# Two lead-ins of a hybrid block: single PSUM banks, and the last chunk's norm set step by step among the weights' splits

## The chip, the cores and the metric

One core of a Trainium2 chip runs the kernel. The metric is the device time of one execution in microseconds (us); the median of three runs before the change is 2560.94, from 2557.63 to 2561.89.

## The reference

One layer of a trunk with three sub-layers on x of shape [1, 1024, 1024] in float32. Each is normalised before and after, and added to the stream:

```python
x = x + rms_norm(merged @ w_mix_out[l], g_post_mix[l])
h = rms_norm(x, g_pre_xa[l])
mem_n = rms_norm(mem, g_mem[l])
x = x + rms_norm(memory_cross_attention(h, mem_n, w_xq[l], w_xkv[l], w_xo[l]), g_post_xa[l])
h = rms_norm(x, g_pre_ffn[l])
x = x + rms_norm(swiglu(h, w_gu[l], w_down[l]), g_post_ffn[l])
```

`merged` is a stick-breaking attention and a Mamba-2 mixer, gated and summed. `memory_cross_attention` begins with the query projection `h @ w_xq`, and `swiglu` with `h @ w_gu`, 1024 to 2 x 2816. The change is about the places where an output projection, a post-norm, an addition and a pre-norm run into one of these two products.

## The kernel before, in words

The engines are TensorE (PE, matmul), VectorE (DVE), ScalarE (ACT), GpSimd (POOL) and SyncE (SP, which issues most transfers). Matrices are split into a high part and a low part of reduced precision (`hi` is made by ACT, `lo` by DVE as the difference), and each product is three matmuls: high by high, high by low, low by high. A weight tile of 128 output columns and half of the 1024 inputs thus needs 12 matmuls of 128x128 by 128x512; this is `acc3`, called a product below.

**The chunks.** `out_proj` (L1453) multiplies the activations by an output projection in chunks of 128 rows, 8 in all, four to a half of the sequence. For each chunk it loads the old x, makes the product in a two-bank PSUM tile (tag `p2`), squares and sums it on ACT (L1469), turns the sum into a scale on POOL (`rstd_of`, L173 and L174), scales by it and by the gain on DVE (L1471, "the first scaling"), adds the old x (L1472), and stores the new x. `pre_norm` (L178) then does a second square (L181) and a second scaling (L182) for the sub-layer that follows, and returns a function that transposes the chunk on PE (8 transposes) and one, `put`, that moves the transposes into the blocks that the next products need (L1513 for the second half: two copies on ACT, six operations on DVE). The list `late` holds these back so that the transposes of a chunk follow the product of the next.

**The scheme of the products.** The next sub-layer's matmul is done by a Winograd-Strassen scheme: of each weight block with quarters a11, a12, a21, a22 it makes combinations s1 = a21 + a22, s2 = s1 - a11, s3 = a11 - a21, s4 = a12 - s2, and of the activations blocks b11, b21, b22, t1, t2, t3, t4. Seven products per 128 columns give the four quarters of the result: in the accumulator pa go a11 x b11, then s2 x t2, s3 x t3 and a22 x t4; in pb a12 x b21; in pc s1 x t1, then s4 x b22. Copies (ACT) and additions (DVE) between them pick up the partial sums.

**The lead-ins.** The first four columns of 128 of each of the two projections are done by `opening` (L1571) and `lead_in` (L1581), in two pairs, so that they can begin before all chunks of the second half are normalised. `opening` makes the first three products, pa[0], pa[1] and pb[0], right behind chunk 7's, with chunk 6's transposes among them. `lead_in` goes on with na[0] and na[1] (the second pair's a11 x b11), the rest of pb, and then `stages` (L1606 on) twice. The names q11 to q22 are the quarters of the first pair's weights and n11 to n22 of the second's.

**What sets the order.** `in_turn(True)` makes DVE, ACT and PE issue their instructions exactly in the order in which the Python code calls them (each call is recorded by a helper, so all have line L49 in the profile). A call that stands early and waits holds everything behind it on its engine. Outside of the lead-ins a scheduler decides. SP's transfers go in the order of its queue, and `behind` sets one after a given instruction.

**Banks.** [...] `bank()` takes one of two single banks (pool `psa`, tag `mm`), and

```python
def two_banks():
    t = mk(psp, [P, 2, HALF], F32, "p2")
    return t[:, 0], t[:, 1]
```

takes one tile of two banks from the pool `psx`, which also serves the chunks' products and their transposes (tag `tr`). In the lead-in pb and na are such tiles. The framework sets waits by tile, so an instruction that writes one half waits for the reader of the other.

**Buffers.** Chunk 7's x goes to a tile `wraw` of the weights' pool, chunks 4 to 6's to the pool `t4` with three tiles (tag `x4`). The query's first weights n11, n12, q12, q21 are loaded into unused halves of the result tiles `qT`; q22 and q11 go to `t4`. The feed-forward's go to `fg`, `fw` and the rotating pool `rp`. Split weights of a lead-in rotate in `swp`, six tiles in the query's and seven in the feed-forward's. Behind the feed-forward's lead-in the loop `strassen` (L1878) does the remaining 18 columns with `winograd_pair` (L246) and `winograd_weights` (L198), which also rotate in `swp`.

The profile's names drop buffer numbers: `qT` is the query's result, `t` and `sw` are results and split weights in the feed-forward, `sf` the combinations, `h` and `tx` the split blocks, `x` and `xk` the chunk and the float32 blocks.

Of the kernel before, what the change touches and what calls it, by code (L numbers as in the profile page):

```python
# [16 lines left out]
P = 128  # L17
# [37 lines left out]
def hybrid_block(ctx, tc, a, out, dbg=None):  # L55
# [122 lines left out]
    def pre_norm(psp, xt, yt, gbc, put):  # L178

        ms = mk(stats, [P, 1], F32, "ms")  # L180
        A.activation(yt, xt, AF.Square, scale=D ** -0.5, accum_out=ms)  # L181
        V.scalar_tensor_tensor(yt, xt, rstd_of(ms), gbc, ALU.mult, ALU.mult)  # L182

        def turns():
            pts = []
            for kh in range(2):
                pts.append(mk(psp, [P, 4, P], F32, "tr"))
                for k in range(4):
                    T.transpose(pts[kh][:, k, :], yt[:, (kh * 4 + k) * P:(kh * 4 + k + 1) * P], ident)
            return lambda: put(pts, yt)  # L190
        return turns
# [1260 lines left out]

    def out_proj(half, act, w, t4, psp, x_src, x_dst, gpost, gpre, put, ahead=None):  # L1453

        wh, wl = w
        for ci in range(4):
            c = half * 4 + ci
            cs = slice(ci * P, (ci + 1) * P)
            xt = mk(t4, [P, D], F32, "x4") if ci < 3 or ahead is None else ahead()
            nc.sync.dma_start(xt, x_src[c * P:(c + 1) * P, :])  # L1460
# [6 lines left out]
            yt = mk(t4, [P, D], F32, "x4")  # L1467
            ms = mk(stats, [P, 1], F32, "ms")
            order = [A.activation(yt, pb, AF.Square, scale=D ** -0.5, accum_out=ms)]  # L1469
            rs = rstd_of(ms)  # L1470
            V.scalar_tensor_tensor(yt, pb, rs, gpost, ALU.mult, ALU.mult)  # L1471
            order.append(V.tensor_tensor(xt, xt, yt, ALU.add))  # L1472
            queue = nc.sync if ahead is None or ci < 2 else nc.scalar
            order.append(queue.dma_start(x_dst[c * P:(c + 1) * P, :], xt))
            marks.append(order)
            if late and (ahead is None or ci < 3):
                late.pop()()()
            late.append(pre_norm(psp, xt, yt, gpre, put(cs)))
# [20 lines left out]
    def first_half(hb, xf):  # L1499
        hb["b11"], hb["b21"] = quad(accp, "a8")  # L1500

        def at(cs):
            def put(pts, yt):
                for nm, pt in zip(("b11", "b21"), pts):
                    hi, lo = [t[:, :, cs] for t in hb[nm]]
                    A.activation(hi, pt, AF.Copy)
                    V.tensor_tensor(lo, pt, hi.bitcast(F32), ALU.subtract)
                for x, pt in zip(xf, pts):
                    A.activation(x[:, :, cs], pt, AF.Copy)
            return put  # L1510
        return at

    def second_half(hb, xf):  # L1513
        hb["b22"], hb["t1"] = quad(h2, "h2")

        def at(cs):
            def put(pts, yt):
                b22, t1 = [[t[:, :, cs] for t in hb[nm]] for nm in ("b22", "t1")]
                x11, x21, x2 = [x[:, :, cs] for x in xf]
                x = yt[:, 0:HALF].rearrange("p (k t) -> p k t", t=P)  # L1520
                A.activation(b22[0], pts[1], AF.Copy)
                V.tensor_tensor(x, pts[0], x11, ALU.subtract)
# [5 lines left out]
                V.tensor_tensor(x21, x21, x2, ALU.subtract)  # L1528
            return put
        return at  # L1530
# [50 lines left out]
    def lead_in(hb, xf, pa, pb, q, nq, sfp, swp, y, n00, ny, last, nlast, open_tx):  # L1581
# [4 lines left out]
        q11, q12, q21, q22 = [pick(r) for r in q]  # L1586
# [73 lines left out]
    with ExitStack() as q1:  # L1660
        gpool = pool(q1, "gx")
        gpost, gpre = load_gain(gpool, "g_post_mix"), load_gain(gpool, "g_pre_xa")
        mg = []
        for half in range(2):
            sl = slice(half * HALF, (half + 1) * HALF)
            mg.append(quad(h2, "h2"))
            for k in range(KT):
                hi, lo = mg[half][k // 4]
                hi_sb(hi[:, k % 4, :], acc[k][:, sl], "a")
                lo_of(lo[:, k % 4, :], acc[k][:, sl], hi[:, k % 4, :])  # L1670
        hx = {}
        xf = fp32_blocks()
        out_proj(0, mg[0], wmix, t4, psp, x_in, x2_d, gpost, gpre, first_half(hx, xf))

        def lead_xq():
            with behind(marks[AFTER_M]):
                lead.extend(lead_weights(wbig, a["w_xq"][0]))
            return mk(wbig, [P, D], F32, "wraw", 2)

        lead = []  # L1680
        out_proj(1, mg[1], wmix, t4, psp, x_in, x2_d, gpost, gpre, second_half(hx, xf), lead_xq)
# [12 lines left out]
    with ExitStack() as q2:  # L1694
# [13 lines left out]
        with ExitStack() as xs:  # L1708
            sfp = pool(xs, "qsf", 4, side="right")
            swp = pool(xs, "qsw", 6, side="right")  # L1710
            tx = pool(xs, "qtx", 2, side="right")
# [5 lines left out]
            def more(kh, c0):  # L1717
                with behind(loads[-1:]):
# [5 lines left out]
            q22, q11 = more(1, 2), more(0, 0)  # L1724
            lead_in(hx, xf, xa, xb, (q11, q12, q21, q22), (n11, n12, lambda: more(0, 6), lambda: more(1, 6)), sfp, swp,
                    rows_of(0), [qT[4 + p][:, 0:HALF] for p in range(2)], lambda: rows_of(4), fourth(2), fourth(6), lambda: tx)
# [66 lines left out]
    with ExitStack() as q3:  # L1793
        gpool = pool(q3, "gx3")
        wbig = pool(q3, "wbigB", 8, side="right")
        wxo = big_weight(wbig, a["w_xo"][0], 2, True)
        gpost, gpre = load_gain(gpool, "g_post_xa"), load_gain(gpool, "g_pre_ffn")
        hw = {}
        xf = fp32_blocks()
        out_proj(0, ox[0], wxo, t4, psp, x2_d, x3_d, gpost, gpre, first_half(hw, xf))  # L1800

        def lead_gu():
            with behind(marks[NCH + AFTER_O]):
                lead.extend(lead_weights(wbig, a["w_gu"][0]))
            return mk(wbig, [P, D], F32, "wraw", 2)

        lead = []
        out_proj(1, ox[1], wxo, t4, psp, x2_d, x3_d, gpost, gpre, second_half(hw, xf), lead_gu)
    fa, fb = opening(hw, lead)


# [7 lines left out]
    with ExitStack() as q4:  # L1819
        t2 = pool(q4, "t2f", 6, side="right")  # L1820
        sfp = pool(q4, "fsf", 4, side="right")
        swp = pool(q4, "fsw", 7, side="right")
# [12 lines left out]
        def load(q, kh, c0):  # L1835
            quarter_load(q, w_gu, kh, c0)
            return quarter(q)
# [14 lines left out]

        def open_tx():
            xt4.close()
            return pool(q4, "tx", 2, side="right")

        fg, fw = [mk(fdp, [P, 2, S], F32, nm) for nm in ("fg", "fw")]
        n11 = load(fg[:, 0], 0, 2 * P)
# [3 lines left out]
        q11 = load(fw[:, 0], 0, 0)  # L1862
        n21 = load(fw[:, 1], 0, FFN + 2 * P)
# [5 lines left out]
        def later_results():  # L1869
# [3 lines left out]
        lead_in(hw, xf, fa, fb, (q11, q12, q21, q22), (n11, n12, lambda: n21, lambda: more(1, FFN + 2 * P)), sfp, swp,  # L1873
                y, n00, later_results, both_gated(y, 0, "xk0"), both_gated(ny, 2, "xk1"), open_tx)
        psx.close()
# [274 lines left out]
```

## Time and profile before

| what | us |
|---|---|
| median of three runs | 2560.94 |
| the profiled execution | 2566.68 |
| its span | 2565.0 |
| PE busy in the span | 2463.0 (96%) |
| DVE, ACT, POOL busy | 1815.1, 1162.9, 827.8 |
| chunk 7's product ends (query, feed-forward) | 1638.0, 1894.4 |
| first product behind the lead-in of the feed-forward | 1988.7 |

Times of the trace are in us from the start of the span; the profiled execution's 2566.68 is the span and 1.7 around it. A row of the timeline gives the start, the length, the engine, the line, the operation with its output and inputs, and in brackets the idle time before it with what ended it. A row that ends in x24 is that many instructions without a break. Matmuls overlap, so a row's length runs a little past the start of what follows. A table by stretch gives busy times between two moments.

### The profile page before, as it was taken

The numbers are of one execution on the slowest core, as the hardware profiler recorded it, in microseconds if no ns is written. First come the engines' busy times: TensorE is split into PE (matmuls) and PEld (weight loads), VectorE is DVE, ScalarE is ACT, GpSimd is POOL, SyncE is SP. The second block draws the span as 40 slices with busy tenths as digits, with TensorE's granted clock in tenths as the row PEclk, the third lists the DMA queues.
The fourth block names the chain that finished last, engine by engine and source line by source line (L and its number), as shares of the span: only waits on it lengthen the run. The fifth ranks groups of instructions, "written<-read, shape, count | busy, mean of one in ns | idle before, by whom it ended". The sixth has DMA issues, their size and how long they took to land. (4 is left out here: it accounts for less than half of the span.)

```text
span 2565.0 us, 33376 instructions
## 1 busy us (share of the span) xinstructions
PE 2463.0 (96%) x12306; PEld 2015.3 (79%) x12306; DVE 1815.1 (71%) x2165; ACT 1162.9 (45%) x2075; POOL 827.8 (32%) x638
## 2 busy tenths in 40 slices
PE   7999999999999999989999999989998999999998
PEld 5788888888788788777777778767776888888876
DVE  7765877766578787698898654656466666666997
ACT  5333555555456565565554203425344333334343
POOL 3221644443211111256565140101111233333662
PEclk9999999999999999999999999999999999999999
DMA  7431433333443443365332642411231222224232
GB/s 246 155 124 58 143 126 108 107 107 115 120 107 99 116 103 92 111 205 167 101 111 72 230 165 74 131 50 50 99 131 62 91 86 74 87 95 164 99 131 99
DMA packets 249133, 295.62 MB, mean 115 GB/s; under 512 B 17023, under 2 KB 169096, under 8 KB 248842
## 3 DMA queue, kind: packets, MB, share of 16 engines
q1 hardware_dynamic: 248394, 291.40, 36.4%
q8 instruction: 97, 1.59, 0.3%
q10 hardware_dynamic: 576, 2.10, 0.2%
q14 instruction: 66, 0.54, 0.1%
HBM read 202.20 MB, written 74.45 MB: 108 GB/s over the span
## 5 line engine op out<-in xcount | busy, mean ns | idle before, releaser
L922 DVE TENSOR_TENSOR_SCAN n<-n,mask 128x128 f32<-128x128 f32 (+7 forms) x128 | 187.6, 1490 | 26.3 <-ACT n L921 25.0
L122 DVE TENSOR_TENSOR sw<-sf,sw 128x512 fp32r<-128x512 f32 x142 | 112.9, 806 | 76.4 <-ACT sw L119 74.7
L939 ACT ACTIVATE wth<-tr,mone 128x512 fp32r<-128x512 f32 x192 | 110.4, 584 | 83.9 <-PE tr L936 83.1
L119 ACT ACTIVATE sw<-sf 128x512 fp32r<-128x512 f32 x142 | 87.5, 627 | 116.9 <-PE mm L241 100.3
L207 POOL TENSOR_TENSOR sf<-wr,wr 128x512 f32<-128x512 f32 x36 | 51.5, 1432 | 268.4 <-DMA wr<-in_w_gu_dram 131.4
L940 DVE SCALAR_TENSOR_TENSOR wtl<-tr,wth 128x512 fp32r<-128x512 f32 x192 | 99.5, 543 | 50.8 <-ACT wth L939 50.5
L122 DVE TENSOR_TENSOR sw<-wr,sw 128x512 fp32r<-128x512 f32 x107 | 104.2, 975 | 26.0 <-ACT sw L119 25.9
L704 DVE SCALAR_TENSOR_TENSOR b<-b,prmT,b 128x1023 f32<-128x1023 f32 (+2 forms) x72 | 109.6, 1522 | 17.0 <-ACT b L698 16.4
L119 ACT ACTIVATE sw<-wr 128x512 fp32r<-128x512 f32 x107 | 67.4, 631 | 110.6 <-PE mm L241 104.3
L115 POOL TENSOR_SCALAR v<-va 128x512 fp32r<-128x512 f32 x16 | 20.5, 1283 | 288.5 <-PE av L949 166.9
L239 PE MATMUL mm<-h,sw 128*128 128x512 f32 x288 | 112.0, 389 | 0.0
L240 PE MATMUL mm<-h,sw 128*128 128x512 f32 x288 | 112.0, 389 | 0.0
L921 ACT ACTIVATE n<-sc 128x512 f32<-128x512 f32 (+1 forms) x192 | 88.7, 493 | 49.0 <-PE tr L936 28.8
L241 PE MATMUL mm<-h,sw 128*128 128x512 f32 x288 | 109.8, 389 | 0.0
L173 POOL TENSOR_SCALAR rstd<-ms 128x1 f32<-128x1 f32 x74 | 29.0, 392 | 240.0 <-ACT x L1469 111.0
L125 PE MATMUL mm<-oth,bw 128*128 128x512 f32 x256 | 103.6, 405 | 2.3 <-DVE a L1261 2.1
L125 PE MATMUL p<-bw,h 128*128 128x512 f32 x256 | 99.6, 394 | 2.4 <-DVE x L1471 2.4
L127 PE MATMUL p<-bw,h 128*128 128x512 f32 x256 | 100.8, 394 | 0.5 <-DVE h L122 0.5
L126 PE MATMUL p<-bw,h 128*128 128x512 f32 x256 | 100.5, 393 | 0.0
L126 PE MATMUL mm<-otl,bw 128*128 128x512 f32 x256 | 100.5, 393 | 0.0
L127 PE MATMUL mm<-oth,bw 128*128 128x512 f32 x256 | 100.5, 392 | 0.0
L936 PE MATMUL tr<-ident,n 128*128 128x128 f32 x576 | 95.3, 275 | 3.1 <-DVE wtl L940 3.1
(671 smaller groups left out, 7967.9 us busy)
## 6 DMA issues: line engine op xcount, KB each, us to landing
wr<-in_w_in_dram SPq DMA_DIRECT2D x36, 512.0 KB
wr<-in_w_gu_dram SPq DMA_DIRECT2D x72, 256.0 KB
zr<-in_w_in_dram SPq DMA_DIRECT2D x28, 512.0 KB
wraw<-in_w_in_dram SPq DMA_DIRECT2D x20, 512.0 KB
gu_d<-t SPq DMA_DIRECT2D x36, 256.0 KB
zs_d<-zo SPq DMA_DIRECT2D x32, 256.0 KB
xs_d<-b SPq DMA_DIRECT2D x32, 256.0 KB
kl<-gt SPq DMA_DIRECT2D x64, 128.0 KB
```

The lines of the kernel that those rows point to most:

```text
L119: A.activation(o, i, AF.Copy)
L122: eng.tensor_tensor(o, i, hi.bitcast(F32), ALU.subtract)
L125: first = T.matmul(ps, sh, mh, start=start, stop=False)
L126: T.matmul(ps, sh, ml, start=False, stop=False)
L127: T.matmul(ps, sl, mh, start=False, stop=stop)
L239: T.matmul(ps, w[0][:, k, :], bh, start=first and k == 0, stop=False, skip_group_check=True)
L240: T.matmul(ps, w[0][:, k, :], bl, start=False, stop=False, skip_group_check=True)
L241: ins = T.matmul(ps, w[1][:, k, :], bh, start=False, stop=last and k == 3, skip_group_check=True)
L704: V.scalar_tensor_tensor(acc[:, sh:], y[:, :S - sh], cw(3 - sh, f), acc[:, sh:], ALU.mult, ALU.add)
L922: V.tensor_tensor_scan(nt[:, 0:L][:, ::-1], nt[:, 0:L][:, ::-1], mask[:, S - L:][:, ::-1], 1.0, ALU.mult, ALU.max)
L939: A.activation(wh[:, t0 * P:], pt[:, t0 * P:], AF.Identity, bias=mone)
L940: V.scalar_tensor_tensor(wl[:, t0 * P:], pt[:, t0 * P:], -1.0, wh[:, t0 * P:].bitcast(F32), ALU.add, ALU.subtract)
```

## The change

The diff's core ("..." marks what is left out):

```diff
-    def pre_norm(psp, xt, yt, gbc, put):
...
+    def mean_square(x, junk):
         ms = mk(stats, [P, 1], F32, "ms")
-        A.activation(yt, xt, AF.Square, scale=D ** -0.5, accum_out=ms)
-        V.scalar_tensor_tensor(yt, xt, rstd_of(ms), gbc, ALU.mult, ALU.mult)
...
+        return ms, A.activation(junk, x, AF.Square, scale=D ** -0.5, accum_out=ms)
...
+        def chunk(ci, xt, pb):
+            c = half * 4 + ci
+            rows = slice(c * P, (c + 1) * P)
+            nc.sync.dma_start(xt, x_src[rows, :])
+            yield
+            yt = mk(t4, [P, D], F32, "x4")
+            ms, square = mean_square(pb, yt)
+            V.scalar_tensor_tensor(yt, pb, rstd_of(ms), gpost, ALU.mult, ALU.mult)
+            yield
+            order = [square, V.tensor_tensor(xt, xt, yt, ALU.add)]
+            queue = nc.sync if ahead is None or ci != 2 else nc.scalar
+            order.append(queue.dma_start(x_dst[rows, :], xt))
+            marks.append(order)
+            ms = mean_square(xt, yt)[0]
+            rs = rstd_of(ms)
+            yield
+            V.scalar_tensor_tensor(yt, xt, rs, gpre, ALU.mult, ALU.mult)
+            yield
...
+            held = ahead is not None and ci == 3
+            if held:
+                ahead()
+            xt = mk(t4, [P, D], F32, "x4")
             pb = mk(psp, [P, D], F32, "p2")
+            run = chunk(ci, xt, pb)
+            if not held:
+                next(run)
...
+            if held:
+                late.append(run)
+                return
+            next(run)
+            next(run)
+            if late:
+                finish(late.pop()())
+            finish(run)
...
                 A.activation(b22[0], pts[1], AF.Copy)
+                yield
                 V.tensor_tensor(x, pts[0], x11, ALU.subtract)
                 A.activation(t1[0], x, AF.Copy)
                 V.tensor_tensor(b22[1], pts[1], b22[0].bitcast(F32), ALU.subtract)
                 V.tensor_tensor(x2, pts[1], x, ALU.subtract)
                 V.tensor_tensor(t1[1], x, t1[0].bitcast(F32), ALU.subtract)
+                yield
                 V.tensor_tensor(x11, x2, x11, ALU.subtract)
                 V.tensor_tensor(x21, x21, x2, ALU.subtract)
+                yield
...
         acc3(pa[0], ws[0], hb["b11"], True, False)
+        late[0] = late[0]()
         acc3(pa[1], ws[1], hb["b11"], True, False)
-        late[0] = late[0]()
         acc3(pb[0], ws[2], hb["b21"], True, True)
...
+            s4 = combined(room(), a12, s2, ALU.subtract)
             block("t3")
-            s4 = combined(room(), a12, s2, ALU.subtract)
...
         n0, n1 = weights(n11)
-        late[0]()
+        put, run = late
+        late.clear()
+        with behind([loaded]):
+            next(run)
+        next(run)
+        next(put)
+        next(run)
+        next(put)
+        finish(run)
+        finish(put)
         first_sum(y[0][0][0], pa[0], pb[0])
-        na = two_banks()
+        psl = open_ps()
+        banks = [mk(psl, [P, HALF], F32, "mm") for _ in range(6)]
+        pb, na = banks[0:2], banks[2:4]
         acc3(na[0], n0, hb["b11"], True, False)
-        put = late[1]()
-        late.clear()
+        put = late.pop()(banks[4:6])
         q1 = split_weight(swp, "sw", q12[1])
-        put()
+        finish(put)
+        q22, q11 = pick(q[3]()), pick(q[0]())
...
+            def open_ps():
+                psx.close()
+                return pool(psl, "psl", 6, PSUM)
...
-        swp = pool(q4, "fsw", 7, side="right")
+        swp = pool(q4, "fsw", 6, side="right")
...
-            p = winograd_pair(psf, winograd_weights(rp, sfp, swp, loads), hw, y)
+            p = winograd_pair(psf, winograd_weights(rp, sfp, swp, loads, firstp=ld), hw, y)
```

It has these parts.

1. **Single banks.** Once the first sum has been recorded, `open_ps` closes the pool of two-bank tiles and opens six single banks: two for pb, two for na, and two for the transposes of chunk 7. pb[0] of the opening still lies in a two-bank tile.
2. **The norm of chunk 7 step by step.** `chunk` is a generator that stops after the load, after the first scaling, after the add (with the store and the second square), and after the second scaling. For chunk 7 `lead_in` runs it, between the splits of n0 and n1 and the two halves of chunk 6's `put`. Chunk 6's transposes go between the first two products.
3. **Transfers.** Chunk 7's x goes to the pool `t4` and is loaded behind the weights (`loaded`); its store goes to SP's queue instead of ACT's. q22 and q11 are loaded where the code now calls for them.
4. **The combination s4** goes ahead of the split of the block t3.
5. **The feed-forward's pools.** `swp` has six tiles, and in the loop `strassen` the splits of a11 and a12 rotate in the two tiles of the pool `ld`.

The first place is DVE's order at the end of the query's chunk 7. In these rows `x_3127` and `x_3138` are chunk 7 before and now, `x_3113` is chunk 6, `p_3126` is chunk 7's product, `sw` low parts of n0 and n1, and `qT<-qT,p` the first sum. DVE before:

```order
L1471 SCALAR_TENSOR_TENSOR x_3127_15360<-p_3126_15311,rstd_15363,g_post_mix_14679 128x1024
L1472 TENSOR_TENSOR wraw_15309<-wraw_15309,x_3127_15360 128x1024
L182 SCALAR_TENSOR_TENSOR x_3127_15360<-wraw_15309,rstd_15371,g_pre_xa_14681 128x1024
L49 TENSOR_TENSOR sw_15450<-qT_3140_15432,sw_15450 128x512
L49 TENSOR_TENSOR sw_15453<-qT_3140_15432,sw_15453 128x512
L49 TENSOR_TENSOR x_3113_15263<-tr_15403,xk_3048_14723 128x512
L49 TENSOR_TENSOR h_3090_15043<-tr_15408,h_3089_15042 128x4x128
L49 TENSOR_TENSOR xk_3050_14725<-tr_15408,x_3113_15263 128x4x128
L49 TENSOR_TENSOR h_3092_15045<-x_3113_15263,h_3091_15044 128x4x128
L49 TENSOR_TENSOR xk_3048_14723<-xk_3050_14725,xk_3048_14723 128x4x128
L49 TENSOR_TENSOR xk_3049_14724<-xk_3049_14724,xk_3050_14725 128x4x128
L49 TENSOR_TENSOR qT_3137_15429<-qT_3137_15429,p_3134_15378 128x512
```

And in the changed kernel:

```order
L49 TENSOR_TENSOR sw_15426<-qT_3135_15415,sw_15426 128x512
L49 TENSOR_TENSOR sw_15429<-qT_3135_15415,sw_15429 128x512
L49 SCALAR_TENSOR_TENSOR x_3138_15433<-p_3126_15310,rstd_15436,g_post_mix_14679 128x1024
L49 TENSOR_TENSOR x_3125_15309<-x_3125_15309,x_3138_15433 128x1024
L49 TENSOR_TENSOR x_3113_15263<-tr_15374,xk_3048_14723 128x512
L49 TENSOR_TENSOR h_3090_15043<-tr_15375,h_3089_15042 128x4x128
L49 TENSOR_TENSOR xk_3050_14725<-tr_15375,x_3113_15263 128x4x128
L49 TENSOR_TENSOR h_3092_15045<-x_3113_15263,h_3091_15044 128x4x128
L49 SCALAR_TENSOR_TENSOR x_3138_15433<-x_3125_15309,rstd_15445,g_pre_xa_14681 128x1024
L49 TENSOR_TENSOR xk_3048_14723<-xk_3050_14725,xk_3048_14723 128x4x128
L49 TENSOR_TENSOR xk_3049_14724<-xk_3049_14724,xk_3050_14725 128x4x128
L49 TENSOR_TENSOR qT_3132_15412<-qT_3132_15412,p_3129_15361 128x512
```

The two low parts moved ahead of the norm, and four operations of chunk 6's put moved between its add and its second scaling; the first sum still stands behind all of it.

The second place is PE at the same moment, printed with the engines whose semaphores each row waits for. `p_3134` and `p_3129` are pb, `p_3145` and `mm_15464` are na[0], and the transposes of chunk 7 are `tr` before and `mm_15466` and `mm_15467` now. PE before, from the last matmul of pb[0]:

```order
L49 MATMUL p_3134_15378<-a_3053_14728,wraw_15306 128x512
L49 MATMUL p_3145_15466<-a_3051_14726,sw_15450 128x512 [waits DVE_49,Activation_49]
...
L49 MATMUL p_3145_15466<-a_3051_14726,sw_15450 128x512
L49 MATMUL tr_15479<-ident_88,x_3127_15360 128x128 [waits DVE_49]
L49 MATMUL tr_15479<-ident_88,x_3127_15360 128x128 x3
L49 MATMUL tr_15484<-ident_88,x_3127_15360 128x128 [waits DVE_49,PE_49]
```

And in the changed kernel:

```order
L49 MATMUL p_3129_15361<-a_3053_14728,wraw_15306 128x512
L49 MATMUL mm_15464<-a_3051_14726,sw_15426 128x512 [waits DVE_49]
...
L49 MATMUL mm_15464<-a_3051_14726,sw_15426 128x512
L49 MATMUL mm_15466<-ident_88,x_3138_15433 128x128 [waits PE_49]
L49 MATMUL mm_15466<-ident_88,x_3138_15433 128x128 x3
L49 MATMUL mm_15467<-ident_88,x_3138_15433 128x128 x4
```

na[0] now waits for DVE's first sum, which reads pb[0] (`p_3129`); since that stands behind chunk 7's second scaling, the transposes have no wait for DVE left.

The third place is SP's queue there: `qT` are the four weight loads, `x_d` the stream in memory, `in_x_dram` the old x. SP before:

```order
L1460 DMA wraw_15309<-in_x_dram 128x1024
L1551 DMA qT_3140_15432<-in_w_xq_dram 128x4x256
L1551 DMA qT_3139_15431<-in_w_xq_dram 128x4x256
L1551 DMA qT_3137_15429<-in_w_xq_dram 128x4x256
L1551 DMA qT_3138_15430<-in_w_xq_dram 128x4x256
L1551 DMA x_3141_15446<-in_w_xq_dram 128x4x256
```

And in the changed kernel:

```order
L1578 DMA qT_3135_15415<-in_w_xq_dram 128x4x256
L1578 DMA qT_3134_15414<-in_w_xq_dram 128x4x256
L1578 DMA qT_3132_15412<-in_w_xq_dram 128x4x256
L1578 DMA qT_3133_15413<-in_w_xq_dram 128x4x256
L1453 DMA x_3125_15309<-in_x_dram 128x1024
L1461 DMA x_d<-x_3125_15309 128x1024
L1578 DMA x_3150_15499<-in_w_xq_dram 128x4x256
```

Chunk 7's load moved behind the four weight loads, and its store, which ACT issued before, now stands between it and the load of q22 (`x_3150`).

More of the change, by code (lines that the diff above doesn't have):

```diff
@@ L1658, in lead_in, with lead_xq @@
         in_turn(False)
[L1660 to L1681, printed above, removed]
+    q1 = ExitStack()
+    gpool = pool(q1, "gx")
+    gpost, gpre = load_gain(gpool, "g_post_mix"), load_gain(gpool, "g_pre_xa")
+    mg = []
+    for half in range(2):
+        sl = slice(half * HALF, (half + 1) * HALF)
+        mg.append(quad(h2, "h2"))
+        for k in range(KT):
+            hi, lo = mg[half][k // 4]
+            hi_sb(hi[:, k % 4, :], acc[k][:, sl], "a")
+            lo_of(lo[:, k % 4, :], acc[k][:, sl], hi[:, k % 4, :])
+    hx = {}
+    xf = fp32_blocks()
+    out_proj(0, mg[0], wmix, t4, psp, x_in, x2_d, gpost, gpre, first_half(hx, xf))
+    def lead_xq():
+        with behind(marks[AFTER_M]):
+            lead.extend(lead_weights(wbig, a["w_xq"][0]))
+    lead = []
+    out_proj(1, mg[1], wmix, t4, psp, x_in, x2_d, gpost, gpre, second_half(hx, xf), lead_xq)
     def bank():
@@ L1723, in hybrid_block @@
             n11, n12, q12, q21 = [load(r, kh, c0) for r, (kh, c0) in zip(spare, ((0, 4), (1, 4), (1, 0), (0, 2)))]
-            q22, q11 = more(1, 2), more(0, 0)
-            lead_in(hx, xf, xa, xb, (q11, q12, q21, q22), (n11, n12, lambda: more(0, 6), lambda: more(1, 6)), sfp, swp,
-                    rows_of(0), [qT[4 + p][:, 0:HALF] for p in range(2)], lambda: rows_of(4), fourth(2), fourth(6), lambda: tx)
+            lead_in(hx, xf, xa, xb, (lambda: more(0, 0), q12, q21, lambda: more(1, 2)), (n11, n12, lambda: more(0, 6), lambda: more(1, 6)), sfp, swp,
+                    rows_of(0), [qT[4 + p][:, 0:HALF] for p in range(2)], lambda: rows_of(4), fourth(2), fourth(6), open_ps, open_tx, loads[-1])
+            psl.close()
+            psx = ExitStack()
+            psp = pool(psx, "psx", 2, PSUM)
         pp = pool(q2, "pp", 4, side="right")
@@ L1791, in hybrid_block, with lead_gu @@
             mix(half, h, ox[half])
[L1793 to L1808, printed above, removed]
+    q3, q3w = ExitStack(), ExitStack()
+    gpool = pool(q3, "gx3")
+    wbig = pool(q3w, "wbigB", 8, side="right")
+    wxo = big_weight(wbig, a["w_xo"][0], 2, True)
+    gpost, gpre = load_gain(gpool, "g_post_xa"), load_gain(gpool, "g_pre_ffn")
+    hw = {}
+    xf = fp32_blocks()
+    out_proj(0, ox[0], wxo, t4, psp, x2_d, x3_d, gpost, gpre, first_half(hw, xf))
+    def lead_gu():
+        with behind(marks[NCH + AFTER_O]):
+            lead.extend(lead_weights(wbig, a["w_gu"][0]))
+    lead = []
+    out_proj(1, ox[1], wxo, t4, psp, x2_d, x3_d, gpost, gpre, second_half(hw, xf), lead_gu)
     fa, fb = opening(hw, lead)
+    q3w.close()
     w_gu, w_dn = a["w_gu"][0], a["w_down"][0]
```

59 lines of the change are left out of this document (27 added, 32 removed).

## The prediction

> **What bounds the kernel now.** I read four views in this order: the page's busy shares, the table of busy time by stretch, the waits of TensorE in the two stretches that the change touches, and the timeline of TensorE there. The page comes first.
>
> ```profile
> PE 2463.0 (96%) x12306; PEld 2015.3 (79%) x12306; DVE 1815.1 (71%) x2165; ACT 1162.9 (45%) x2075; POOL 827.8 (32%) x638
> ```
>
> TensorE (PE) is busy 96% of the span, so the end is its work plus its waits. The table by stretch says where the other 4% lie; after the stretch's bounds and length come the busy times of PE, weight loads, VectorE (DVE), ScalarE (ACT) and GpSimd (POOL), then PE's granted clock.
>
> ```profile
> 1638.00:1740.00 102.00, 89.02 (x373) 69.78 (x372) 54.58 (x78) 33.76 (x56) 2.63 (x5) 0.97 0.20 67
> 1894.00:1990.00 96.00, 83.57 (x361) 65.19 (x360) 66.27 (x93) 40.99 (x67) 12.87 (x12) 1.00 0.22 73
> 1988.00:2400.00 412.00, 411.44 (x1815) 340.38 (x1814) 269.47 (x316) 156.50 (x263) 135.69 (x86) 1.00 0.31 102
> ```
>
> The first is the lead-in of the query projection, the second that of the feed-forward, the third the steady loop behind it. Both lead-ins leave PE idle for over 12 us; the steady loop for 0.6. The waits of PE in the three stretches (total us, times, longest):
>
> ```profile
> PE p L49 <- DVE qT L49: 7.4, 6, 2.2
> PE p L49 <- ACT qT L49: 3.8, 4, 1.7
> PE mm L49 <- ACT qT L49: 1.5, 1, 1.5
> PE p L1751 <- ACT qT L49: 0.3, 1, 0.3
> ...
> PE p L49 <- DVE t L49: 5.8, 4, 2.2
> PE p L49 <- ACT t L49: 3.4, 4, 1.2
> PE p L49 <- DVE sw L49: 2.2, 2, 1.4
> PE p L49 <- ACT sw L119: 0.9, 1, 0.9
> PE p L49 <- ACT sw L49: 0.2, 1, 0.2
> ...
> PE mm L239 <- DVE t L270: 0.6, 1, 0.6
> ```
>
> Nearly every wait is one of `p`, the two-bank tile. The engine waited for is the one that reads the product made just before: PE wants to start in one bank and is held by the reader of the other.
>
> How much could go? These rows of the timeline (start, length, what, wait ahead of it) are the query's, then the feed-forward's.
>
> ```profile
> 1638.02 5.61 PE L49 MATMUL mm<-a,sw 128*128 128x512 f32 x24
> 1647.08 2.91 PE L49 MATMUL p<-a,sw 128*128 128x512 f32 x12
> 1658.17 4.61 PE L49 MATMUL p<-a,sw 128*128 128x512 f32 x12 [1.85 <-DVE qT L49]
> 1691.91 4.58 PE L49 MATMUL p<-h,sw 128*128 128x512 f32 x12 [2.23 <-DVE qT L49]
> 1732.48 2.75 PE L1751 MATMUL p<-xk,qT 128*128 128x256 f32 x12
> 1734.88 3.12 PE L49 MATMUL p<-tx,sw 128*128 128x512 f32 x12
> 1737.85 0.59 PE L1751 MATMUL p<-xk,qT 128*128 128x256 f32 x2
> ```
>
> ```profile
> 1894.44 5.61 PE L49 MATMUL mm<-a,sw 128*128 128x512 f32 x24
> 1915.37 3.01 PE L49 MATMUL p<-a,sw 128*128 128x512 f32 x12 [1.90 <-DVE t L49]
> 1930.27 11.04 PE L49 MATMUL mm<-h,sw 128*128 128x512 f32 x48
> 1941.15 2.88 PE L49 MATMUL p<-h,sw 128*128 128x512 f32 x12
> 1946.26 2.99 PE L49 MATMUL p<-h,sw 128*128 128x512 f32 x12 [2.23 <-DVE t L49]
> 1988.70 0.39 PE L239 MATMUL mm<-a,sw 128*128 128x512 f32 x1
> ```
>
> Four products of 12 matmuls without a wait take 1941.15 - 1930.27 = 10.88, so 2.72 each. A lead-in makes 28 of them (four columns of weights, seven products each), and two sets of eight transposes; the first three products with one such set take 1647.08 - 1638.02 = 9.06, so a set is 0.9. Undisturbed, a lead-in needs 28 x 2.72 + 1.8 = 78.0. The query's took 1737.85 - 1638.02 = 99.83, less 2.40 for the L1751 scores put in between (1734.88 - 1732.48), so 97.4: **19.4 lost**. The feed-forward's took 94.3: **16.3 lost**. Together 35.7. That is more than the listed waits (12.7 and 12.5) because a wait is counted from the modelled end, 0.28 after the next product could have started (3.00 against 2.72), in about twelve places each, and because of the half clock below.
>
> **The change part by part.** *Single banks.* Each product of a lead-in now has a bank of its own, so PE no longer waits for the neighbour's reader. By itself this removes the waits of `p`. It leaves true ones: a bank is used again after two products, so its reader has one product, 2.7 us, in which to finish.
>
> *The s4 combination ahead of the split of t3.* The one wait of `mm`, 1.5 us, is PE waiting for ACT's copy, which stood behind a DVE combination. It goes; it is in the 19.4.
>
> *The order of the last chunk's norm, and a new wait.* In the changed program the product na0 (the first into `mm_15464`) gets a bank that pb0 held, so it must wait for the first sum, which reads pb0. That sum stands on DVE behind the whole norm chain of chunk 7. Before, na0 didn't wait for that sum. The steps of the chain, DVE's and then ACT's:
>
> ```profile
> 1640.33 1.28 DVE L1471 SCALAR_TENSOR_TENSOR x<-p,rstd,g_post_mix 128x1024 f32<-128x1024 f32 x1 [2.02 <-POOL rstd L174]
> 1641.65 1.23 DVE L1472 TENSOR_TENSOR wraw<-wraw,x 128x1024 f32<-128x1024 f32 x1
> 1645.42 1.28 DVE L182 SCALAR_TENSOR_TENSOR x<-wraw,rstd,g_pre_xa 128x1024 f32<-128x1024 f32 x1 [2.55 <-POOL rstd L174]
> 1650.22 1.29 DVE L49 TENSOR_TENSOR xk<-xk,xk 128x512 f32<-128x512 f32 x2
> 1651.43 0.68 DVE L49 TENSOR_TENSOR qT<-qT,p 128x512 f32<-128x512 f32 x1
> ...
> 1638.22 1.03 ACT L1469 ACTIVATE x<-p 128x1024 f32<-128x1024 f32 x1 [2.49 <-PE p L127]
> 1643.28 1.06 ACT L181 ACTIVATE x<-wraw 128x1024 f32<-128x1024 f32 x1 [3.94 <-DVE wraw L1472]
> 1644.34 1.14 ACT L49 ACTIVATE sw<-qT 128x512 fp32r<-128x512 f32 x2
> ```
>
> From the end of chunk 7 (T = 1638.0): the square begins 0.2 later, and now 1.0 later still, since two high parts of weights (the last row, 1.14 for both, of which 0.1 lies under its neighbours) stand ahead of it on ACT; 2.11 from the square to the first scaling (1638.22 to 1640.33); 1.32 to the add; 1.63 to the second square; 2.14 to the second scaling; 1.2 for that; 1.2 for two subtractions; 0.7 for the sum and PE's start. T + 11.5. PE is there at T + 9.1. So **na0 waits 2.4 us** in each lead-in, and the transposes of chunk 7, queued behind it, are then ready. The four put operations that now stand between add and second scaling (2.4 us at 0.60 each, the step from 1650.22 to 1651.43 being two) fit into the 2.55 that DVE waited there. Behind na0 on PE stand the transposes, na1 and pb1; DVE's put of chunk 7 waits for those and starts 2.4 us later than PE alone would allow. pb1 then ends at T + 20.9, and from there DVE has eight operations of 0.60 to the sum that frees pc0's bank: T + 25.7, and PE wants it at T + 26.0. It holds, barely.
>
> *Transfers.* The square of chunk 7 now writes a buffer that chunk 6's store reads, so it also waits for that store. SyncE's queue shows when the store landed before:
>
> ```profile
> SPq L1551 <- DMA x_d<-x: 8.9, 1, 8.9
> ...
> 1630.66 0.34 SPq L1460 DMA_DIRECT2D wraw<-in_x_dram  x1
> 1642.63 12.92 SPq L1551 DMA_DIRECT2D x<-in_w_xq_dram  x3
> ```
>
> At T + 4.5, with five loads of 512 KB (chunk 7's x, the first row, and four of weights) issued ahead of it. Now chunk 7's x comes last instead of first. A sixth of the 12 us from that issue to the landing is 2 us, by which the store should land sooner; that is an estimate. Bounds of na0's wait: 0 if the norm's order turned out free, 2.4 + 3.3 = 5.7 if the store lands as late as before. I take **2.7 each**, near the chain's own length. The store of chunk 7 goes to SyncE, ahead of the q22 load (first of the three above): it would leave at about T + 6 instead of T + 4.6, and its first use stands over 15 us later on DVE. No cost while that cover lasts; without it, a load's 2 to 3 us.
>
> *Steady loop.* The first splits for it are moved into the feed-forward's lead-in, and two of seven weight pairs get the pool of `ld`; eight slots instead of seven. I cost this at nothing: PE waits 0.6 us in 412 there, and DVE is busy 269. Bounds: -0.6 and the fourth rival. The feed-forward's lead-in, though, holds 66.3 us of DVE work in what becomes 82, 81% busy: some of the 8.0 us of waits for DVE there should stay. Bounds 0 and 8.0; I take 2.0, nearer nothing because the trace blames most of them on the other bank.
>
> *The clock.* Two blocks of the query took 4.6 instead of 3.0; at the first and at the like place of the feed-forward:
>
> ```profile
> 1658.60:1662.10 3.50, 3.50 (x11) 2.69 (x10) 3.28 (x6) 2.38 (x5) 0.00 (x0) 0.53 0.00 0
> 1911.00:1919.00 8.00, 5.48 (x23) 3.87 (x22) 7.90 (x14) 3.82 (x8) 0.00 (x0) 1.00 0.00 0
> ```
>
> Half clock for about 3.4 us after gaps of 1.85 and 2.23; none after gaps of 1.90 and 2.23 in the feed-forward. So a gap of 2 us may or may not cost 1.6 more. The gap before na0 may bring one back: half of 1.6, 0.8. [...]
>
> **Sum.** 35.7 - 2 x 2.7 (na0) - 2 x 0.3 (its restarts) - 0.8 (clock) - 2.0 (DVE in the feed-forward) = 26.9 us. The profiled execution took 2566.68 and should become 2539.8. The median of the runs is 2560.94, 0.2% lower; the same microseconds off give **2534 us**.
>
> **The rivals.**
> 1. *The store is as late as before*: chunk 7's chain is held at both places, na0 waits 5.7. For it: 8.9 us of waiting in SyncE's row. Against: one load fewer ahead. 26.9 - 6.0 = 20.9: 2540.
> 2. *DVE becomes the bound*: banks come free, but its order holds PE where DVE is named, and only the eight waits for ACT's copies go (3.8 + 3.4, and 8 x 0.28): 9.4 us, 2551.5. For it: 81% in the feed-forward, 0.3 us of slack at pc0. Against: in the longest waits DVE had nothing to do but the reading.
> 3. *The half clock stays in the query*, wherever the gaps go: 3.2 instead of 0.8, so 24.5 off, 2536.5.
> 4. *Slower: the steady loop starts to wait.* Its weights' splits come in another order and in rotating slots of another pool; if a product finds its low part late once per pass, with the 2.2 us that such a wait took in a lead-in, 18 passes cost 40 us and the time is 2574. It decides from 26.9 / 18 = 1.5 us per pass. Against: DVE is idle 35% of that stretch, and ACT 62%.
> 5. *It doesn't do what it says*: the banks end up bound to the same readers as before, and gaps of the same sum stand elsewhere: 2561.
>
> **How the numbers follow.** Forecast 0.50, rivals 0.14, 0.16, 0.08, 0.08, 0.04. Faster: the first four, 0.88. The low end is every loss gone, 2561 - 36 = 2525, less one for the runs' spread: 2524. The high end takes in the second rival: 2553. Left out are the last two, 0.12, and some of each edge. About 0.2%, 5 us, is what a measurement can tell from no change here.
>
> **What would show it.** In the changed profile: PE's waits in the query's lead-in fall from 13 to about 3 to 4 us, with one wait of 2 to 3 named for DVE's first sum about 9 us after chunk 7, and no wait of `mm` for ACT's copy at 1.5. The lead-ins take about 82 and 84 us. The square of chunk 7 starts 1 to 2 us after its last matmul; 4 would be rival 1. The steady loop keeps its 0.6 us. I am wrong if na0 starts without a wait, if waits for DVE's splits and sums of over a microsecond remain at several places, or if any regular wait shows in the steady loop.

## The result, and the profile after

The changed kernel takes 2534.24 us (median of four runs, 2529.46 to 2536.13) against 2561.41 before (four runs, 2557.63 to 2563.15): a ratio of 0.9893, 95% interval 0.9875 to 0.9911, or 27.2 us less. The forecast was 2534, within 2524 to 2553. The profiled execution took 2529.46, 4.8 below the median, where that of before lay 5.3 above its own; so the two traces differ by 37.2 us, and only a part of that is the change. One of the four runs of sum_first_2 below took 2725.46 us at a granted clock of 0.85 instead of 0.995; its median is of the other three.

The page and the table by stretch of the changed kernel: the feed-forward's lead-in and the steady loop, in the columns shown before.

```profile
PE 2452.0 (97%) x12306; PEld 2013.9 (80%) x12306; DVE 1802.7 (71%) x2165; ACT 1164.9 (46%) x2075; POOL 818.6 (32%) x638
...
1869.00:1965.00 96.00, 93.51 (x419) 76.76 (x418) 74.72 (x104) 45.31 (x76) 14.69 (x13) 1.00 0.31 102
1965.00:2377.00 412.00, 411.67 (x1817) 340.62 (x1816) 256.25 (x317) 158.91 (x263) 135.81 (x92) 1.00 0.31 104
```

PE's busy time in the 96 us of the feed-forward's stretch rises from 83.6 to 93.5, since the waits are gone and it reaches the steady loop sooner. The waits of PE, first the query's lead-in, then the feed-forward's, then the steady loop:

```profile
PE mm L49 <- DVE qT L49: 2.3, 1, 2.3
...
PE mm L49 <- DVE t L49: 2.2, 1, 2.2
PE mm L230 <- DVE sw L122: 0.3, 1, 0.3
...
PE mm L228 <- DVE t L259: 0.3, 1, 0.3
```

Of ten lines and some 25 us two waits are left in the lead-ins, one in each, and two of 0.3 us in the loop behind. The timeline of PE shows where. The query's lead-in first, then the feed-forward's:

```profile
1631.76 2.89 PE L49 MATMUL mm<-a,sw 128*128 128x512 f32 x12
...
1638.09 2.88 PE L49 MATMUL p<-a,wraw 128*128 128x512 f32 x12
1643.26 3.06 PE L49 MATMUL mm<-a,sw 128*128 128x512 f32 x12 [2.29 <-DVE qT L49]
1646.16 1.03 PE L49 MATMUL mm<-ident,x 128*128 128x128 f32 x8
1646.95 11.14 PE L49 MATMUL mm<-a,sw 128*128 128x512 f32 x48
1657.95 22.05 PE L49 MATMUL mm<-h,sw 128*128 128x512 f32 x96
...
1712.49 10.88 PE L1798 MATMUL p<-xk,qT 128*128 128x256 f32 x48
...
1871.21 2.89 PE L49 MATMUL mm<-a,sw 128*128 128x512 f32 x12
...
1882.59 3.02 PE L49 MATMUL mm<-a,sw 128*128 128x512 f32 x12 [2.17 <-DVE t L49]
...
1951.79 0.39 PE L228 MATMUL mm<-a,sw 128*128 128x512 f32 x1
```

The row with the wait is na0, right behind pb0 (`p<-a,wraw`), and behind it PE runs without a gap: 96 matmuls in one row, where before most rows had 12 or 24 and the longest 48. The query's lead-in takes 1712.49 - 1631.76 = 80.7 us instead of 97.4, the feed-forward's 1951.79 - 1871.21 = 80.6 instead of 94.3. That is 16.7 and 13.7, together 30.4 us. Chunk 7 of the query also ends 6.3 us sooner in this execution (1631.8 against 1638.0), ahead of the lead-in; I put that down to the two executions. Up to 3.4 of it is an estimate from the granted clock, which was 0.50 for 3.41 us four times ahead of that moment in before (from 75.0, 662.1, 1085.4 and 1167.3 on) and twice in the changed kernel (from 1082.4 and 1246.2 on). In the other eight traces chunk 7 ends between 1631.1 and 1635.0, in banks_only, whose code up to there is that of before, at 1633.1.

The chain of chunk 7's norm in the query, DVE's rows and then ACT's and SyncE's:

```profile
1635.23 1.28 DVE L49 SCALAR_TENSOR_TENSOR x<-p,rstd,g_post_mix 128x1024 f32<-128x1024 f32 x1 [1.31 <-POOL rstd L174]
...
1640.12 1.28 DVE L49 SCALAR_TENSOR_TENSOR x<-x,rstd,g_pre_xa 128x1024 f32<-128x1024 f32 x1
1641.32 1.29 DVE L49 TENSOR_TENSOR xk<-xk,xk 128x512 f32<-128x512 f32 x2
1642.52 0.68 DVE L49 TENSOR_TENSOR qT<-qT,p 128x512 f32<-128x512 f32 x1
...
1633.12 1.03 ACT L49 ACTIVATE x<-p 128x1024 f32<-128x1024 f32 x1
...
1621.54 5.89 SPq L1578 DMA_DIRECT2D qT<-in_w_xq_dram  x4
1629.34 0.34 SPq L1453 DMA_DIRECT2D x<-in_x_dram  x1
```

The square starts 1.4 us after chunk 7's product, the second scaling follows the put operations on DVE without a wait, and the first sum ends at T + 11.4 (1643.2), where the forecast's chain had T + 11.5. The four weight loads left from 1621.5 on, 10 us ahead of the end of chunk 7; before, the row of the same loads stood behind chunk 7's x, which itself left only 7.4 us ahead of it.

### The profile page after: what moved, and what is told of

It is laid out like the page before. It is cut to its first block, busy times and chain, and to the rows that moved or that the text cites. A ratio compares the mean times of both kernels' runs of the same rounds, so it can differ in the third digit from the quotient of the medians.

```text
span 2527.7 us, 33384 instructions
## 1 busy us (share of the span) xinstructions
PE 2452.0 (97%) x12306; PEld 2013.9 (80%) x12306; DVE 1802.7 (71%) x2165; ACT 1164.9 (46%) x2075; POOL 818.6 (32%) x638
## 3 DMA queue, kind: packets, MB, share of 16 engines
q10 hardware_dynamic: 288, 1.05, 0.1%
## 5 line engine op out<-in xcount | busy, mean ns | idle before, releaser
L122 DVE TENSOR_TENSOR sw<-sf,sw 128x512 fp32r<-128x512 f32 x142 | 127.4, 901 | 70.2 <-ACT sw L119 68.1
L199 POOL TENSOR_TENSOR sf<-wr,sf 128x512 f32<-128x512 f32 x36 | 57.8, 1607 | 107.5 <-issue 85.6
```

The lines of the kernel that those rows point to most:

```text
L122: eng.tensor_tensor(o, i, hi.bitcast(F32), ALU.subtract)
```

## The experiments

The theory after the result: **the single banks carry the gain, and the order of the norm lets them carry more of it**, since the product na0 waits for a sum that stands behind that norm. The rival: the order carries it and the banks little. Lead-ins are given in us, query and feed-forward, from the first product of the opening to the row behind the last, without the scores that are put in between; each wait is that of the row shown.

| kernel | time, us | lead-ins | wait of na0 |
|---|---|---|---|
| before | 2561.4 | 97.4, 94.3 | none |
| changed | 2534.2 | 80.7, 80.6 | 2.3, 2.2 |
| banks_only | 2544.6 | 86.8, 86.8 | 4.9, 5.7 |
| order_only | 2559.9 | 93.5, 94.5 | none |
| swap_banks (one run) | 2532.5 | 80.8, 80.6 | 2.3, 2.2 |
| sum_first | 2534.2 | 79.7, 81.6 | 1.3, 3.2 |
| sum_first_2 | 2530.7 | 80.8, 79.5 | 2.4, 1.1 |
| load_first (one run) | 2537.9 | 86.3, 84.2 | 6.0, 4.3 |
| s4_back (one run) | 2535.2 | 83.1, 80.6 | 2.9, 2.2 |
| slots (one run) | 2532.4 | 80.8, 80.7 | 2.4, 2.3 |

**banks_only.** The kernel before with single banks alone.

```diff
-        na = two_banks()
+        psl = open_ps()
+        banks = [mk(psl, [P, HALF], F32, "mm") for _ in range(6)]
+        pb, na = banks[0:2], banks[2:4]
...
-        put = late[1]()
+        put = late[1](banks[4:6])
```

> The kernel before with nothing but the six single banks in the lead-ins (norm of chunk 7, transfers, s4 and pools as before). Theory A, the banks carry the gain: the many waits of p go, but the product na0 now waits for the first sum, which here stands behind the old norm order and ended 14.1 us after chunk 7 in the trace of before, against 9.1 for PE: 5 us in each lead-in; the 1.5 us wait for ACT's copy behind s4 stays in the query. Gain 35.7 - 2 x 5.3 - 1.8 = 23: about 2538 to 2541. Rival B, the order of the norm carries it: gain 10 or less, 2551 or more, with waits of 1 to 2 us left at several products.

Measured 2544.55, ratio 0.9929 (0.9916 to 0.9943): 17 us of the 27. Its timeline of PE at na0, and at the place behind s4, query first:

```profile
1647.23 4.61 PE L49 MATMUL mm<-a,sw 128*128 128x512 f32 x12 [4.93 <-DVE qT L49]
1676.22 11.17 PE L49 MATMUL mm<-h,sw 128*128 128x512 f32 x48 [1.53 <-ACT qT L49]
...
1894.36 5.49 PE L49 MATMUL mm<-a,sw 128*128 128x512 f32 x12 [5.72 <-DVE t L49]
```

The two waits are where the first theory had them, at 4.9 and 5.7 us for 5. What it missed are the rows' lengths: 12 matmuls took 4.6 and 5.5 us instead of 3.0. In the feed-forward the granted clock was 0.50 from 1893.4 on (the last section has the rows); the query's 4.61 is as long as the rows over which it was 0.50 in the trace of before (4.61 and 4.58). The rival is out: with the old order the banks give most of the gain.

**order_only.** The changed kernel with two-bank tiles.

```diff
-        psl = open_ps()
-        banks = [mk(psl, [P, HALF], F32, "mm") for _ in range(6)]
-        pb, na = banks[0:2], banks[2:4]
+        na = two_banks()
...
-        put = late.pop()(banks[4:6])
+        put = late.pop()()
```

> The changed kernel with two-bank tiles put back in the lead-ins (all other parts of the change kept). Theory A: the waits of p come back one after each product as before; only the 1.5 us wait for ACT's copy and perhaps 2 to 4 us at the start of the lead-ins go: 2553 to 2558. Rival B: the order carries the gain: 2545 or less. na0 should not wait for the first sum, since it gets chunk 7's tile.

Measured 2559.88, ratio 0.9988 (0.9979 to 0.9997): 1.9 us less than the median of 2561.73 of before beside it, a smaller gain than either theory gave. Its waits come back one behind another; five of PE's rows in the query:

```profile
1653.09 3.04 PE L49 MATMUL p<-a,sw 128*128 128x512 f32 x12 [0.85 <-DVE qT L49]
1657.55 3.06 PE L49 MATMUL p<-a,sw 128*128 128x512 f32 x12 [1.42 <-DVE qT L49]
1661.45 3.02 PE L49 MATMUL p<-h,sw 128*128 128x512 f32 x12 [0.85 <-DVE qT L49]
1665.15 3.01 PE L49 MATMUL p<-h,sw 128*128 128x512 f32 x12 [0.69 <-ACT qT L49]
1683.99 4.57 PE L49 MATMUL p<-h,sw 128*128 128x512 f32 x12 [2.23 <-DVE qT L49]
```

The wait of `mm` for ACT's copy behind s4 is gone, as foretold, and the 0.85s and 0.69s are those of before. 17 and 2 don't add up to 27. The table shows where the other 8 lie: with the rest of the change na0's wait is shorter by 2.6 and 3.5 than in banks_only, and the 12 matmuls behind it take 3.1 and 3.0 (1.6 and 2.5 more in banks_only). That is 10 us in the traces, and it can be won only where the banks are single, since with two-bank tiles na0 has no such wait. The 1.5 of s4 isn't part of it: it goes with either kind of bank and is among the 2 of order_only.

**swap_banks.** pb and na exchanged among the new banks.

```diff
-        pb, na = banks[0:2], banks[2:4]
+        pb, na = banks[2:4], banks[0:2]
```

> The changed kernel with pb and na exchanged among the six new banks. My prediction said that na0 waits 2.3 us because its bank is the one that pb0 held. Theory A, it is the bank: the wait goes, a lead-in takes 78.3 instead of 80.7 us, and the time falls by 4.6 to about 2530. Rival B, it is the hand-over of the whole pool (the new pool may be written only once all readers of the old one are done): the wait of 2.3 us stays at the first product into the new pool, 2534.

```profile
1646.52 3.04 PE L49 MATMUL mm<-a,sw 128*128 128x512 f32 x12 [2.34 <-DVE qT L49]
...
1885.96 3.02 PE L49 MATMUL mm<-a,sw 128*128 128x512 f32 x12 [2.15 <-DVE t L49]
```

PE's na0 in both lead-ins: the wait stays. It isn't na0's bank that holds it: pb0 can lie under only one of the two pairs, and with either na0 waits for the sum. That leaves the hand-over: `open_ps` closes the old pool, and the first product into the new one waits until all of the old has been read. This follows from two arrangements and the code; a kernel in which na0 needs no new pool wasn't tried.

**sum_first.** The first sum two subtractions earlier on DVE.

```diff
         finish(run)
-        finish(put)
         first_sum(y[0][0][0], pa[0], pb[0])
+        finish(put)
```

> The changed kernel with the first sum ahead of the last two subtractions of chunk 6's put on DVE (two operations of 0.60 us fewer ahead of it). Theory A, na0's wait is set by the sum's place on DVE: 2.3 becomes 1.1 in each lead-in, and the time falls by 2.4 to about 2532. Rival B, what stands behind holds next (the transposes, or the sum that frees pc0's bank, with 0.3 us of slack by the prediction): the wait moves and the time stays at 2534.

Measured 2534.20, ratio 0.9887 (0.9874 to 0.9901): no gain. PE's na0 in both, then ACT's square of chunk 7 in the feed-forward:

```profile
1644.91 3.04 PE L49 MATMUL mm<-a,sw 128*128 128x512 f32 x12 [1.26 <-DVE qT L49]
1885.21 3.02 PE L49 MATMUL mm<-a,sw 128*128 128x512 f32 x12 [3.17 <-DVE t L49]
...
1876.29 1.02 ACT L49 ACTIVATE x<-p 128x1024 f32<-128x1024 f32 x1 [2.11 <-DMA x_d<-x]
```

In the query the wait falls by 1.0, as the theory has it. In the feed-forward it grows by 1.0, and ACT's row says why: the square waits 2.1 us for chunk 6's store. Outside of the lead-ins a scheduler sets the order, and with this edit it set chunks 4 to 6 of the feed-forward's output projection differently: chunk 6's second scaling starts at 1873.19, 0.4 us behind chunk 7's product, where in the changed kernel it starts at 1868.22, 3.0 us ahead of it. Its store, which comes before that scaling, leaves 2.5 us ahead of the end of chunk 7's product (1870.36) instead of 5.9 (1865.34). That is my first rival, not taken by the change but one edit away.

**sum_first_2.** The same idea, with the scheduler's order as in the changed kernel; `early` is set in the feed-forward only.

```diff
                 V.tensor_tensor(x11, x2, x11, ALU.subtract)
+                yield
                 V.tensor_tensor(x21, x21, x2, ALU.subtract)
...
         finish(run)
-        finish(put)
+        if not early:
+            next(put)
         first_sum(y[0][0][0], pa[0], pb[0])
+        finish(put)
```

> The changed kernel with the first sum one subtraction earlier in the query and two earlier in the feed-forward; unlike in sum_first, the order of chunks 4 to 6 of the feed-forward's output projection is that of the changed kernel. Theory A: the sum's place on DVE sets na0's wait, and what spoilt sum_first in the feed-forward was the later store of chunk 6. Then na0 waits 1.7 us in the query (2.3 less 0.6) and 1.0 in the feed-forward (2.2 less 1.2), the square of chunk 7 starts 1.3 us after its product in both, and the time falls by 1.8 to about 2532.4. Rival B: the feed-forward's sum is held by something else and its wait stays at 2.2 or grows to 3.

Measured 2530.66 (three runs), ratio 0.9880 (0.9860 to 0.9900). PE's na0 in both, then ACT's square in the query:

```profile
1644.06 3.06 PE L49 MATMUL mm<-a,sw 128*128 128x512 f32 x12 [2.38 <-DVE qT L49]
1882.48 3.02 PE L49 MATMUL mm<-a,sw 128*128 128x512 f32 x12 [1.14 <-DVE t L49]
...
1634.53 1.03 ACT L49 ACTIVATE x<-p 128x1024 f32<-128x1024 f32 x1 [0.71 <-DMA x_d<-x]
```

The feed-forward's wait halves as expected: the sum's place sets it. In the query 0.6 us were to go, but the square waited 0.7 for the store, which landed 2.1 us after chunk 7's product; in the changed kernel's trace no wait for it shows. So the query's wait swings by what the transfers do. By the medians this is the fastest kernel here, but its interval and the changed kernel's overlap, so it isn't shown to beat it.

**load_first.** Chunk 7's x ahead of the weights.

```diff
             run = chunk(ci, xt, pb)
-            if not held:
-                next(run)
+            next(run)
...
-        with behind([loaded]):
-            next(run)
         next(run)
         next(put)
```

> The changed kernel with chunk 7's x loaded ahead of the weights, as before. In the query it waits for its buffer until 2.4 us before chunk 7's product ends, and the four weight loads behind it on SP's queue leave only then. Theory A, the place in the queue matters little here: the store of chunk 6 lands sooner, n0's load a little later; na0 waits 2.3 to 3.3 us, no other wait over 1 us, time 2534 to 2536. Rival B, the later weights hold the splits of n0 and then pb1: waits of 2 us or more at further products of the query, 2538 or more.

```profile
1646.33 4.90 PE L49 MATMUL mm<-a,sw 128*128 128x512 f32 x12 [6.03 <-DVE qT L49]
1889.45 4.54 PE L49 MATMUL mm<-a,sw 128*128 128x512 f32 x12 [4.28 <-DVE t L49]
...
1635.16 1.15 ACT L49 ACTIVATE sw<-qT 128x512 fp32r<-128x512 f32 x2 [4.84 <-DMA qT<-in_w_xq_dram]
...
1630.01 0.34 SPq L1453 DMA_DIRECT2D x<-in_x_dram  x1
1630.39 2.16 SPq L1577 DMA_DIRECT2D qT<-in_w_xq_dram  x4
```

PE's na0 in both, ACT's high parts of n0 and n1 in the query, and SyncE's loads there. Both theories were off. The first put n0's load "a little later"; the four loads left only 0.7 us ahead of the end of chunk 7's product (1631.1), where in the changed kernel they left 10 us ahead, and ACT's row shows n0's high part held until 1635.2, 4.1 us after chunk 7's product, and the whole norm stands behind it on ACT. na0 waits 6.0 and 4.3 us, the 12 matmuls behind each gap take 4.9 and 4.5 us instead of 3.0, and the lead-ins lose 5.6 and 3.6. The waits of the second theory, at further products, don't appear. So the place of one load in SyncE's queue moves na0's wait by more (3.7 and 2.1 us) than the sum's place does (1.0). It also corrects my theory: this kernel has the new order of the norm, yet in the query na0 waits longer than in banks_only (6.0 against 4.9), which has the old one. There the new order pays only together with the new place of the load. In the feed-forward the scheduler's order differs as in sum_first, but the wait there is named for the weights' load too (5.0 us).

**s4_back and slots.** The combination s4 behind the split of t3 again, and the steady loop with six tiles:

```diff
-            s4 = combined(room(), a12, s2, ALU.subtract)
             block("t3")
+            s4 = combined(room(), a12, s2, ALU.subtract)
```

```diff
-            p = winograd_pair(psf, winograd_weights(rp, sfp, swp, loads, firstp=ld), hw, y)
+            p = winograd_pair(psf, winograd_weights(rp, sfp, swp, loads), hw, y)
```

> The changed kernel with the combination s4 behind the split of t3 again. Theory A: PE's wait of 1.5 us for ACT's copy comes back in the query, as in banks_only, and none in the feed-forward: 2536. Rival B: with the other parts in place ACT and DVE are far enough ahead and nothing waits: 2534.

> The changed kernel without the two tiles of ld in the steady loop: all seven weight pairs of a pass rotate in six tiles. Theory A, the slots are not on the path: the loop's waits stay under 1 us in 412 and the time at 2534. Rival B, the split of a22 or of the next a11 waits for a tile that PE still reads: a wait in each of 18 passes, 0.5 us or more each, 2543 or more.

The row of s4_back's PE in the query, and the only wait of PE in slots' steady loop:

```profile
1672.85 11.17 PE L49 MATMUL mm<-h,sw 128*128 128x512 f32 x48 [1.53 <-ACT qT L49]
```

```profile
PE mm L228 <- DVE t L259: 0.6, 1, 0.6
```

The first theories hold in the traces: the 1.5 us come back in the query only, and the eight slots are worth nothing that the trace shows (one wait of 0.6 us in the loop with six tiles; with eight 0.3 there and 0.3 in its first pass). One run each is too few to tell the times apart.

## Why the prediction was right, point by point

- **What bounds the kernel, and 35.7 us to be had.** Right. Less na0's wait and its restart of 0.3, the feed-forward's lead-in is 80.6 - 2.5 = 78.1; the forecast's undisturbed length was 78.0.
- **Single banks remove the waits of p.** Right, and shown by both halves: alone they take 17 us off, and without them the waits are back one by one.
- **The s4 wait.** Right, in place and size (1.53 in s4_back).
- **The new wait of na0.** Right in place and size: the chain gave 2.4, the trace 2.29 and 2.17; the 2.7 that I took, for a late store, was a little high. Wrong in its cause: the prediction said that na0 "gets a bank that pb0 held", and swap_banks shows that another bank changes nothing (2.34 and 2.15). That its size came out right all the same is partly luck: the hand-over of the pool, which is what remains as the cause, waits for the same sum.
- **Transfers.** Right that the store would land sooner, but I counted only one load fewer ahead of it. The store of chunk 7 had left at T + 4.9 before, not at T + 4.6, and leaves at T + 6.0 now, as forecast. The weight loads themselves left 3 us sooner against chunk 7's end, being no longer behind an x that waited for its buffer. load_first prices the place at 5.6 + 3.6 = 9 us in the two lead-ins of its trace (its one run took only 3.7 more than the changed kernel's median); the prediction priced only a late store, at 6 for both.
- **The feed-forward's DVE, 2.0 us.** Mis-sized: 0.3 is left, at the first pass of the loop. The busy share of 81% made me keep some waits, though the rows already named the other bank.
- **The clock, 0.8 us.** Mis-sized: none in the lead-ins, where the granted clock was 1.00 behind na0's gaps of 2.29 and 2.17 too. The last section has the rows of the first.
- **The steady loop at nothing.** Right: 0.6 us of waits before, and now 0.3 besides the 0.3 of the first pass.
- **The sum.** 26.9 forecast, 27.2 by the medians, 30.4 in the two lead-ins of the traces. Of the 35.7 us to be had the forecast left 8.8 lost, and the two traces left 35.7 - 30.4 = 5.3: about 0.4 and 0.5 less at na0, 0.8 less of the clock, 1.7 less of DVE. The lead-ins were forecast at about 82 and 84 us and took 80.7 and 80.6. So the medians' agreement to 0.3 us is partly luck; runs of one kernel differ by up to 7.6 (before, 15 runs).
- **The rivals.** The store's landing (the first) decided sum_first's feed-forward; DVE as the bound (the second) does not show in any kernel with single banks beyond na0's sum; the third fell with the half clock, which no lead-in of the changed kernel's trace shows (granted clock 1.00 in both); the fourth and fifth don't appear.

## What to carry to other kernels

A tile is what waits are set by: two accumulators in one tile make the matmul engine wait for the reader of the one while it wants to write the other, and here single banks alone took off 17 us, the rest of the change alone 1.9. When a pool is handed over, find the last reader of the old one and how long a chain stands ahead of it: here the first write to the new one waited for that reader with either pair of banks. A load that must wait for its buffer belongs behind those that need not, and an edit in a hand-ordered stretch should be followed into the stretches that a scheduler orders.

## What the runs showed of the hardware

**The clock at the gaps.** In the trace of before the granted clock was 0.50 in two stretches of 3.41 us in the query's lead-in, from 1658.80 and from 1692.93 on, and 1.00 in the whole of the feed-forward's. Rows of the table by stretch: two gaps of 1.85 and 2.23 us with the stretch at 0.50 behind each, then two stretches of the same length over the feed-forward's gap of 2.23.

```profile
1655.38:1658.80 3.42, 1.56 (x8) 0.97 (x7) 3.42 (x7) 0.17 (x2) 0.00 (x0) 1.00 0.49 153
1658.80:1662.21 3.41, 3.41 (x10) 2.64 (x9) 3.08 (x5) 2.44 (x5) 0.00 (x0) 0.50 0.00 0
1689.52:1692.93 3.41, 1.18 (x6) 0.87 (x6) 2.24 (x3) 0.00 (x0) 0.69 (x1) 1.00 0.46 154
1692.93:1696.34 3.41, 3.41 (x10) 2.64 (x9) 1.22 (x1) 0.00 (x0) 0.37 (x1) 0.50 0.25 41
1942.10:1945.51 3.41, 1.93 (x9) 1.27 (x7) 3.41 (x5) 0.00 (x0) 0.00 (x0) 1.00 0.24 73
1945.51:1948.93 3.42, 2.67 (x12) 2.24 (x13) 0.60 (x2) 0.00 (x0) 0.00 (x0) 1.00 0.29 86
```

In the two stretches ahead of the half clock PE was idle for 1.86 and 2.23 us; in the two over the third gap it was idle for 1.48 and 0.75, and the clock stayed at 1.00. And the changed kernel at na0:

```profile
1638.80:1642.21 3.41, 2.17 (x10) 1.48 (x8) 3.41 (x6) 1.68 (x5) 0.79 (x2) 1.00 0.55 190
1642.21:1645.62 3.41, 2.36 (x10) 1.95 (x11) 1.60 (x3) 0.00 (x0) 0.00 (x0) 1.00 0.80 250
```

The gap of 2.29 lies in both stretches, 1.24 of it in the first and 1.05 in the second, and the clock stayed at 1.00. So of these four gaps two were followed by half clock, each at a cost of 1.6 us (12 matmuls took 4.6 instead of 3.0), and two cost nothing more. What decides between them was not shown.

In banks_only's feed-forward, where na0 waits 5.7 us, two such stretches at 0.50 follow each other:

```profile
1889.97:1893.38 3.41, 0.00 (x0) 0.00 (x0) 3.41 (x7) 1.64 (x3) 0.00 (x0) 1.00 0.88 299
1893.38:1896.79 3.41, 2.44 (x6) 1.95 (x7) 1.52 (x3) 0.00 (x0) 0.00 (x0) 0.50 0.00 1
1896.79:1900.21 3.42, 3.42 (x11) 2.64 (x10) 0.00 (x0) 0.00 (x0) 0.00 (x0) 0.50 0.00 0
```

Of the two, PE was idle for 0.97 us of the first and not at all in the second, and the 12 matmuls of na0 took 5.49 us there instead of 3.0, 2.5 longer.
